# Three passes of rounded parts for the mixer's products with v and with the state in the second layer of a four-layer hybrid model

## The chip, the cores and the metric

The kernel runs on one core of one Trainium2 chip. The metric is the device time of one execution in microseconds (us), lower is better; a kernel's time is the median of its runs. The outputs are fp32.

## What is computed

The model has four layers on 1040 tokens (16 meta tokens and 1024 tokens of input) of width 1024: sliding-window attention, an mLSTM, an HGRN2 and attention again. Each layer projects the normed input, mixes over time, gates, and projects back. The change is in the second layer, whose mixer does this for each of 8 heads and for each block of 128 tokens in turn:

```python
def step(carry, inp):                      # mlstm_chunkwise, one block
    C, n, m = carry
    q_, k_, v_, li, lf = inp
    ...
    qk = jnp.einsum('bhtd,bhsd->bhts', q_, k_) * jnp.exp(D - m_t[..., None])
    num = w_inter[..., None] * jnp.einsum('bhtd,bhde->bhte', q_, C) + jnp.einsum('bhts,bhse->bhte', qk, v_)
    den = w_inter * jnp.einsum('bhtd,bhd->bht', q_, n) + qk.sum(axis=-1)
    h = num / jnp.maximum(jnp.abs(den), jnp.exp(-m_t))[..., None]
    ...
    C_new = w_old[..., None, None] * C + jnp.einsum('bhs,bhsd,bhse->bhde', w_s, k_, v_)
```

q and k have 128 columns a head, v has 256. After it, h is multiplied by a sigmoid gate, normed over the head's 256 columns, multiplied by a silu gate and projected by w_out.

## The kernel before, in words

**Staging.** Activations lie with features on the partitions and tokens along the row. Tokens go in three chunks (400, 384, 256) for projections and in nine blocks (16, then eight of 128) for mixers. A projection (`proj` L212, `proj_v` L249, `proj_out` L297) takes both operands as two rounded parts in fp32r, high and low: `split` (L194) makes the high part with ScalarE and the remainder with VectorE, and three passes (high·high, high·low, low·high) are accumulated in one PSUM bank (L231, L281, L326). Weights come by DMA in halves of 512 columns into `raw` (two buffers, L207), and are split into `wh` and `wl` (three buffers each). All DMAs of the layer are issued by SyncE, in order.

**Order.** TensorE's order is written out by hand: lists of steps, each with a cost in nanoseconds, a function that issues it, and perhaps a function `pre` that loads its weights, called as soon as the steps ahead cost less than 12 us (`LOOKAHEAD`). `weave` (L58) merges two lists in proportion to their costs. The other engines' instructions are put in order by the framework's scheduler, by priority; steps wrapped in `hi` (L290) get a priority 40 places earlier.

**The mixer** (`mixer`, L980). `start` loads the head's two decay rows, spread over all 128 partitions (`rb` and `wb`, 1040 columns each, one buffer each, L986 and L987). Then for block b:

- `s1(b)`: q·k on TensorE (L994), k transposed (L996), the decay matrix E (L998 on VectorE, L1000 on ScalarE), W = E times q·k (L1004), qw = q times the row of `wb` (L1007), kw = the transposed k scaled by a column of E (L1012, ScalarE).
- `s2(b)`: num = W·v (L1019) + qw·C (L1021), 257 columns: 256 of v and one of ones that gives the denominator; then the division (L1023 to L1029).
- `s3(b)`: kw·v (L1035), and the new state C = old C times a scalar + that product (L1038 and L1040, VectorE; two buffers).
- `s4(b)`: the result transposed back (L1049, L1051).

The steps go s1(b), s2(b-1), s3(b-1), s4(b-2). All three products L1019, L1021 and L1035 have fp32 operands. A head's mixer list, without its last three steps, is woven with the projections of the next head (q, k, v). The last three are woven with the first six steps of the gate part: `gates` (L1114) gives the two sigmoid-gate projections (`og_proj`, L1065) one after the other, then a silu-gate projection with the three norm statistics (`stat`, L1088) put into it. The second silu gate and `proj_out` follow. For head 6 the last three mixer steps are held over to head 7, whose mixer is woven with head 6's gates. The squares of the first sigmoid-gate half stay in a row of their own, `sqr` (L1076), until the second half adds to it (L1082).

Of the kernel before, what the change touches and what calls it, by code (L numbers as in the profile page):

```python
# [9 lines left out]
F32 = mybir.dt.float32  # L10
F32R = mybir.dt.float32r
# [4 lines left out]
P = 128  # L16
# [57 lines left out]
def flat(groups):  # L74
    return [x for grp in groups for x in grp]
# [38 lines left out]
def hybrid_kernel(ctx: ExitStack, tc: tile.TileContext, ins, out, layers=(0, 1, 2, 3)):  # L114
# [13 lines left out]
    def nm(x):  # L128
        ctr[0] += 1
        return f"{x}{ctr[0]}"  # L130
# [16 lines left out]
    def psum(tag, bufs):  # L147
        return ps.tile([P, 512], F32, tag="p", name=nm(tag), bufs=8)
# [141 lines left out]
    def hi(fn):  # L290
        def f():
            with tc.high_priority(offset=PRIO):
                fn()

        return f
# [567 lines left out]
    def layer_b(i, j, fin):  # L863
# [107 lines left out]
        def v_evac(h):  # L971
            def f(acc, b, c0, cn):
                R["v", h, b] = V = vtile()
                put_v(V, acc, b, cn)
                if h == 0:
                    gate_evac(acc, b, cn)
                g.memset(V[:cn, 256:257], 1.0)
            return f

        def mixer(h):  # L980
            W = {}

            def start():
                R["h", h, 0], R["h", h, 1] = row(), row()
                R["rb"], R["wb"] = (R["mix"].tile([P, T], F32, tag=z, name=nm(z), bufs=1) for z in ("rb", "wb"))
                sp.dma_start(R["rb"], R["rows_d"][0, h].partition_broadcast(P))  # L986
                sp.dma_start(R["wb"], R["rows_d"][1, h].partition_broadcast(P))  # L987

            def s1(b):
                mix, q, k = R["mix"], R["q", h], R["k", h]  # L990
                c0, cn = blk(b)
                cs = slice(c0, c0 + cn)
                pq = psum("pm", 2)
                pe.matmul(pq[:cn, :cn], k[:, cs], q[:, cs], start=True, stop=True)  # L994
                if b < NB - 1:
                    pe.transpose(pq[:cn, 128:256], k[:, cs], ident)  # L996
                W["E", b] = E = mix.tile([P, P], F32, tag="E", name=nm("E"), bufs=2)
                v.scalar_tensor_tensor(E[:cn, :cn], R["rb"][:cn, cs], R["bcol"][:cn, b, h : h + 1],  # L998
                                       R["caus"][:cn, :cn], op0=ALU.add, op1=ALU.add)
                s.activation(E[:cn, :cn], E[:cn, :cn], AF.Exp)  # L1000
                W["W", b] = w = mix.tile([P, P], F32, tag="W", name=nm("W"), bufs=2)
                if b == 0:
                    g.memset(w, 0.0)
                v.tensor_tensor(w[:cn, :cn], E[:cn, :cn], pq[:cn, :cn], op=ALU.mult)  # L1004
                if b:
                    W["qw", b] = qw = mix.tile([P, P], F32, tag="qw", name=nm("qw"), bufs=2)
                    v.tensor_tensor(qw, q[:, cs], R["wb"][:, cs], op=ALU.mult)  # L1007
                if b < NB - 1:
                    W["kw", b] = kw = mix.tile([P, P], F32, tag="kw", name=nm("kw"), bufs=2)
                    if b == 0:  # L1010
                        g.memset(kw, 0.0)
                    s.activation(kw[:cn], pq[:cn, 128:256], AF.Identity, scale=E[:cn, cn - 1 : cn])  # L1012

            def s2(b):
                mix = R["mix"]
                c0, cn = blk(b)
                V = R["v", h, b]
                num = psum("po", 1)
                pe.matmul(num[:, :257], W["W", b], V[:, :257], start=True, stop=(b == 0))  # L1019
                if b:  # L1020
                    pe.matmul(num[:cn, :257], W["qw", b], W["C"][:, :257], start=False, stop=True)  # L1021
                den = small(1)
                s.activation(den[:cn], num[:cn, 256:257], AF.Abs)  # L1023
                v.tensor_tensor(den[:cn], den[:cn], R["em"][:cn, b, h : h + 1], op=ALU.max)
                v.reciprocal(den[:cn], den[:cn])
                W["hn", b] = hn = mix.tile([P, 256], F32, tag="hn", name=nm("hn"), bufs=2)
                if b == 0:
                    g.memset(hn, 0.0)
                s.activation(hn[:cn], num[:cn, :256], AF.Identity, scale=den[:cn])  # L1029

            def s3(b):
                mix = R["mix"]
                c0, cn = blk(b)
                pc = psa()
                pe.matmul(pc[:, :257], W["kw", b], R["v", h, b][:, :257], start=True, stop=True)  # L1035
                Cn = mix.tile([P, 258], F32, tag="C", name=nm("C"), bufs=2)
                if b == 0:
                    v.tensor_copy(Cn[:, :257], pc[:, :257])  # L1038
                else:
                    v.scalar_tensor_tensor(Cn[:, :257], W["C"][:, :257], R["wb"][:, c0 + cn - 1 : c0 + cn],  # L1040
                                           pc[:, :257], op0=ALU.mult, op1=ALU.add)
                W["C"] = Cn

            def s4(b):
                c0, cn = blk(b)
                cs = slice(c0, c0 + cn)
                pt = psum("pt", 1)
                for c in range(2):
                    pe.transpose(pt[:, c * P : c * P + P], W["hn", b][:, c * P : c * P + P], ident)  # L1049
                for c in range(2):  # L1050
                    v.tensor_copy(R["h", h, c][:, cs], pt[:, c * P : c * P + cn])  # L1051

            steps = [[0.0, start, None]]
            for b in range(NB + 2):
                if b < NB:
                    steps.append([320, hi(lambda b=b: s1(b)), None])
                if 0 <= b - 1 < NB:
                    steps.append([856, hi(lambda b=b - 1: s2(b)), None])
                    if b - 1 < NB - 1:
                        steps.append([428, hi(lambda b=b - 1: s3(b)), None])  # L1060
                if 0 <= b - 2 < NB:
                    steps.append([214, hi(lambda b=b - 2: s4(b)), None])
            return steps

        def og_proj(h):  # L1065
            st = {}

            def evac(c):
                def f(acc, n, c0, cn):
                    cs = slice(c0, c0 + cn)  # L1070
                    hr = R["h", h, c]
                    a = sigmoid_from(acc[:, :cn], cn)
                    v.tensor_tensor(hr[:, cs], hr[:, cs], a[:, :cn], op=ALU.mult)
                    if c == 0:
                        if n == 0:
                            R["sqr"] = R["mix"].tile([P, T], F32, tag="sqr", name=nm("sqr"), bufs=1)  # L1076
                        R["sq", n] = q = R["sqr"][:, cs]
                        s.activation(q, hr[:, cs], AF.Square)
                    else:
                        q = R["sq", n]  # L1080
                        s.activation(a[:, :cn], hr[:, cs], AF.Square)
                        v.tensor_tensor(q, q, a[:, :cn], op=ALU.add)  # L1082
                        R["sqs", n] = qs = [tpool.tile([P, 400], F32R, tag=z, name=nm(z), bufs=YS)[:, :cn]
                                            for z in ("yh", "yl")]
                        split(q, *qs)
                return f

            def stat(n, c0, cn):  # L1088
                def fn():
                    cs = slice(c0, c0 + cn)  # L1090
                    q = R["sq", n]
                    sm = psa()
                    for i, z in enumerate(R["sqs", n]):
                        pe.matmul(sm[:, :cn], R["ones"], z, start=(i == 0), stop=(i == 1))
                    rstd_from(sm, q, cn, 256)
                    for c in range(2):
                        hr = R["h", h, c]
                        v.scalar_tensor_tensor(hr[:, cs], hr[:, cs], R["hgain"][:, 2 * h + c : 2 * h + c + 1], q,
                                               op0=ALU.mult, op1=ALU.mult)
                return [2 * cn * MM, fn, None]  # L1100

            g0, g1 = (proj(win[8 * h + 4 + c], evac(c)) for c in range(2))
            return g0, g1, [stat(n, *CHUNKS[n]) for n in range(3)]
# [10 lines left out]
        def gates(h):  # L1114
            g0, g1, stats = og[h]
            tail = flat(zg[h][0])
            for n in (2, 1, 0):
                later(tail, (7000.0, stats[n]))
                tail = g1[n] + tail
            return flat(g0) + tail  # L1120

        head = [list(vg[0][n]) for n in range(3)]
        for n in (0, 1):
# [521 lines left out]
```

## Time and profile before

| | |
|---|---|
| runs of the kernel before | 2597.77, 2593.03, 2597.73 us; median 2597.73 |
| the profiled execution | 2594.76 us, its span 2593.0 us |
| second layer, first to last matmul of its mixers | about 544 to 1457 us of the span |
| one head of it (start of one mixer to the next) | 132.8 us, of which the mixer takes about 63 |

The span is what the profiler saw from the first to the last instruction. Engines are PE (TensorE's matmuls), PEld (its weight loads), DVE (VectorE), ACT (ScalarE), POOL (GpSimd), SP (SyncE). A busy time of PE counts each matmul from its start to its modelled end, so neighbours overlap; how much time one really takes on TensorE is seen from the distance between starts, or from the chain of waits, where pieces follow one another. A product with fp32 operands leaves two records, a pass in fp32r one.

### The profile page before, as it was taken

The numbers are of one execution on the slowest core, as the hardware profiler recorded it, in microseconds if no ns is written. First come the engines' busy times: TensorE is split into PE (matmuls) and PEld (weight loads), VectorE is DVE, ScalarE is ACT, GpSimd is POOL, SyncE is SP. The second block draws the span as 40 slices with busy tenths as digits, with TensorE's granted clock in tenths as the row PEclk, the third lists the DMA queues.
The fourth block names the chain that finished last, engine by engine and source line by source line (L and its number), as shares of the span: only waits on it lengthen the run. The fifth ranks groups of instructions, "written<-read, shape, count | busy, mean of one in ns | idle before, by whom it ended". The sixth has DMA issues, their size and how long they took to land.

```text
span 2593.0 us, 54342 instructions
## 1 busy us (share of the span) xinstructions
PE 2547.2 (98%) x20446; PEld 2487.2 (96%) x20446; DVE 1949.5 (75%) x5266; ACT 1682.9 (65%) x4403; POOL 243.4 (9%) x564
## 2 busy tenths in 40 slices
PE   8999999999999999999999999999999999999999
PEld 8899999999999999999999999999999999999999
DVE  7897898785657474747475688978878978887996
ACT  8766766576464555555555757877676857767772
POOL 0321231000000000000000000001000000321330
PEclk9999999999999999999999999999999999999999
DMA  5223212021111111111111111111111113212112
GB/s 157 62 66 95 57 43 70 29 67 54 46 50 49 51 41 58 42 50 45 53 42 50 58 35 34 35 35 35 34 42 34 35 51 93 64 43 82 56 42 78
DMA packets 86058, 140.21 MB, mean 54 GB/s; under 512 B 12425, under 2 KB 39186, under 8 KB 85794
## 3 DMA queue, kind: packets, MB, share of 16 engines
q1 hardware_dynamic: 85794, 136.73, 17.1%
q8 instruction: 161, 2.64, 0.4%
q14 instruction: 103, 0.84, 0.1%
HBM read 121.83 MB, written 4.27 MB: 49 GB/s over the span
## 4 chain that ended last, share of the span: by engine, by line
PE 62%; DVE 13%; ACT 8%; issue 2%; DMA 1%; SPq 0%; POOL 0%; DVEq 0%; ACTq 0%; POOLq 0%
PE pj L231 28%; PE pj L326 14%; PE pj L281 10%; DVE wl L196 1%; PE po L1019 1%; PE po L1021 1%; PE pa L1035 1%; ACT X L1269 1%; PE po L773 1%; DVE x L329 1%; PE pj L277 1%; ACT Sm L737 1%; PE pt L755 1%; DVE Sm L734 1%; DVE X L1267 1%
## 5 line engine op out<-in xcount | busy, mean ns | idle before, releaser
L231 PE MATMUL pj<-uh,wh 128*128 128x256 f32 (+2 forms) x2688 | 915.7, 341 | 7.7 <-ACT uh L401 7.2
L231 PE MATMUL pj<-ul,wh 128*128 128x256 f32 (+2 forms) x2688 | 864.3, 322 | 0.3
L231 PE MATMUL pj<-uh,wl 128*128 128x256 f32 (+2 forms) x2688 | 864.6, 322 | 0.0
L231 PEld LDWEIGHTS pj<-uh,wh 128*128 128x128 f32 x2688 | 508.5, 189 | 17.4 <-ACT uh L401 7.2
L231 PEld LDWEIGHTS pj<-ul,wh 128*128 128x128 f32 x2688 | 508.8, 189 | 6.4 <-DVE ul L196 0.8
L231 PEld LDWEIGHTS pj<-uh,wl 128*128 128x128 f32 x2688 | 507.9, 189 | 0.0
L196 DVE TENSOR_TENSOR wl<-wr,wh 128x512 fp32r<-128x512 f32 (+1 forms) x338 | 234.2, 703 | 55.0 <-ACT wh L195 52.1
L195 ACT CAST wh<-wr 128x512 fp32r<-128x512 f32 (+1 forms) x338 | 202.7, 613 | 97.6 <-PE pj L326 31.5
L326 PE MATMUL pj<-yh,wh 128*128 128x384 f32 (+2 forms) x768 | 253.6, 330 | 9.8 <-DVE x L329 8.3
L329 DVE TENSOR_TENSOR x<-x,pj 128x384 f32<-128x384 f32 (+2 forms) x480 | 233.8, 507 | 33.4 <-PE pj L326 32.1
L326 PE MATMUL pj<-yh,wl 128*128 128x384 f32 (+2 forms) x768 | 246.2, 321 | 0.0
L326 PE MATMUL pj<-yl,wh 128*128 128x384 f32 (+2 forms) x768 | 246.2, 321 | 0.0
L281 PE MATMUL pj<-wh,uh 128*128 128x256 f32 (+1 forms) x768 | 232.7, 303 | 0.0
L281 PE MATMUL pj<-wl,uh 128*128 128x256 f32 (+1 forms) x768 | 216.3, 282 | 0.0
L281 PE MATMUL pj<-wh,ul 128*128 128x256 f32 (+1 forms) x768 | 215.9, 281 | 0.0
L737 ACT ACTIVATE Sm<-Sm,s 128x257 f32<-128x257 f32 (+2 forms) x272 | 131.1, 483 | 88.6 <-DVE s L734 86.3
L740 POOL TENSOR_TENSOR Sm<-Sm,s 128x512 f32<-128x512 f32 (+2 forms) x136 | 139.3, 1024 | 406.5 <-DVE s L739 386.3
L458 ACT ACTIVATE t<-t 128x384 f32<-128x384 f32 (+2 forms) x240 | 118.0, 491 | 75.5 <-DVE t L457 74.6
L195 ACT CAST yh<-r 128x384 fp32r<-128x384 f32 (+2 forms) x120 | 57.0, 478 | 156.2 <-PE pj L326 139.4
L326 PEld LDWEIGHTS pj<-yh,wh 128*128 128x128 f32 x768 | 144.9, 189 | 14.0 <-DVE x L329 10.3
L457 DVE SCALAR_TENSOR_TENSOR t<-pj,t 128x400 f32<-128x400 f32 (+2 forms) x168 | 86.3, 513 | 81.5 <-ACT t L456 80.2
L281 PEld LDWEIGHTS pj<-wh,uh 128*128 128x128 f32 x768 | 144.7, 188 | 2.2
(303 smaller groups left out, 5447.1 us busy)
## 6 DMA issues: line engine op xcount, KB each, us to landing
wr<-in_b_win SPq DMA_DIRECT2D x124, 256.0 KB, 2.8
wr<-in_a_win SPq DMA_DIRECT2D x80, 256.0 KB, 2.8
wr<-in_c_win SPq DMA_DIRECT2D x64, 256.0 KB, 3.0
wr<-in_a_wout SPq DMA_DIRECT2D x32, 256.0 KB, 2.8
wr<-in_b_wout SPq DMA_DIRECT2D x32, 256.0 KB, 2.7
t<-t SPq DMA_DIRECT2D x100, 48.0 KB, 1.9
cs<-in_rope SPq DMA_DIRECT2D x11, 400.0 KB, 3.7
cs<-in_rope SPq DMA_DIRECT2D x11, 384.0 KB, 3.5
```

The costliest lines, as they stand in the source:

```text
L195: s.copy(h, src)
L196: v.tensor_tensor(l, src, h.bitcast(F32), op=ALU.subtract)
L231: pe.matmul(acc[:, :cn], a[:, k, :], b[:, k, c0 : c0 + cn], start=(k == 0 and i == 0), stop=(k == KT - 1 and i == 2))
L277: pe.matmul(acc[:48, :nc], um[0][:, k, :], m[:, kk, :], start=(k == 0 and m is wh), stop=(k == KT - 1 and m is wl))
L281: pe.matmul(acc[:cn, :nc], a[:, k, c0 : c0 + cn], m[:, kk, :], start=(k == 0 and j == 0), stop=(k == KT - 1 and j == 2))
L326: pe.matmul(acc[:, :cn], a[:, k, mc], b, start=(k == 0 and i == 0), stop=(k == 1 and i == 2))
L329: v.tensor_tensor(x[:, m, c0 : c0 + cn], x[:, m, c0 : c0 + cn], acc[:, :cn], op=ALU.add)
L457: v.scalar_tensor_tensor(a[:, :cn], z, 0.0, a[:, :cn], op0=ALU.min, op1=ALU.subtract)
L458: s.activation(a[:, :cn], a[:, :cn], AF.Exp)
L734: v.tensor_tensor_reduce(Sm[:nq, u, :nk], S[:nq, u, :nk], R["masks"][:nq, P + mo : P + mo + nk], rq, sinks[u], ALU.add, ALU.min, st[:nq, u ...
L737: s.activation(Sm[:nq, u, : nk + 1], Sm[:nq, u, : nk + 1], AF.Exp, scale=-1.0, bias=st[:nq, u : u + 1], accum_out=den[:nq, u : u + 1])
L740: g.tensor_tensor(Sm[:nq, :, :nk], Sm[:nq, :, :nk], den[:nq].rearrange("p (u c) -> p u c", c=1).to_broadcast([nq, 2, nk]), op=ALU.mult)
```

## The change

The three products with v and with the state run as three passes over rounded parts, with 258 columns in place of 257 (the ones column is doubled). For this v, W, qw and C are split by `split`, and kw is made as two parts: ScalarE writes the high part in place of kw, VectorE the remainder. The low parts and high parts have tiles of their own (two buffers, for C one), and C is updated in place. The decay rows come block by block (`fetch`, both rows of 128 columns in one DMA, three buffers, block b+1 asked for in s1(b)) in place of `rb` and `wb`, the row `sqr` goes (its use is taken by the rotating buffers of `tmp`), and the two sigmoid gates alternate chunk by chunk in place of one after the other. The costs of s2 and s3 in the list go from 856 and 428 to 714 and 357.

```diff
             def start():
                 R["h", h, 0], R["h", h, 1] = row(), row()
-                R["rb"], R["wb"] = (R["mix"].tile([P, T], F32, tag=z, name=nm(z), bufs=1) for z in ("rb", "wb"))
-                sp.dma_start(R["rb"], R["rows_d"][0, h].partition_broadcast(P))
-                sp.dma_start(R["wb"], R["rows_d"][1, h].partition_broadcast(P))
+                fetch(0)
+
+            def fetch(b):
+                c0, cn = blk(b)
+                W["rw", b] = z = R["mix"].tile([P, 2, P], F32, tag="rw", name=nm("rw"), bufs=3)
+                sp.dma_start(z[:, :, :cn], R["rows_d"][:, h, c0 : c0 + cn].partition_broadcast(P))
+
+            def parts(z, cols=P, bufs=2):
+                return [R["mix"].tile([P, cols], F32R, tag=z + q, name=nm(z + q), bufs=bufs) for q in "hl"]
+
+            def product(acc, a, c, start, stop):
+                for i, (x0, x1) in enumerate(((0, 0), (0, 1), (1, 0))):
+                    pe.matmul(acc, a[x0], c[x1][:, :258], start=(start and i == 0), stop=(stop and i == 2))
 
             def s1(b):
 ...
+                if b + 1 < NB:
+                    fetch(b + 1)
+                rb, wb = (W["rw", b][:, z, :cn] for z in range(2))
+                W["V", b] = parts("V", 258)
+                split(R["v", h, b][:, :258], *(z[:, :258] for z in W["V", b]))
 ...
-                W["W", b] = w = mix.tile([P, P], F32, tag="W", name=nm("W"), bufs=2)
+                w = mix.tile([P, P], F32, tag="W", name=nm("W"), bufs=2)
 ...
                 v.tensor_tensor(w[:cn, :cn], E[:cn, :cn], pq[:cn, :cn], op=ALU.mult)
+                W["W", b] = parts("W")
+                split(w, *W["W", b])
                 if b:
-                    W["qw", b] = qw = mix.tile([P, P], F32, tag="qw", name=nm("qw"), bufs=2)
-                    v.tensor_tensor(qw, q[:, cs], R["wb"][:, cs], op=ALU.mult)
+                    qw = mix.tile([P, P], F32, tag="W", name=nm("qw"), bufs=2)
+                    v.tensor_tensor(qw, q[:, cs], wb, op=ALU.mult)
+                    W["qw", b] = parts("qw")
+                    split(qw, *W["qw", b])
 ...
-                    s.activation(kw[:cn], pq[:cn, 128:256], AF.Identity, scale=E[:cn, cn - 1 : cn])
+                    last = E[:cn, cn - 1 : cn]
+                    s.activation(kh[:cn], pq[:cn, 128:256], AF.Identity, scale=last)
+                    v.scalar_tensor_tensor(kl[:cn], pq[:cn, 128:256], last, kh[:cn].bitcast(F32),
+                                           op0=ALU.mult, op1=ALU.subtract)
 
             def s2(b):
 ...
-                pe.matmul(num[:, :257], W["W", b], V[:, :257], start=True, stop=(b == 0))
+                product(num[:, :258], W["W", b], W["V", b], True, b == 0)
                 if b:
-                    pe.matmul(num[:cn, :257], W["qw", b], W["C"][:, :257], start=False, stop=True)
+                    product(num[:, :258], W["qw", b], W["Cs"], False, True)
 ...
             def s3(b):
 ...
-                pe.matmul(pc[:, :257], W["kw", b], R["v", h, b][:, :257], start=True, stop=True)
-                Cn = mix.tile([P, 258], F32, tag="C", name=nm("C"), bufs=2)
+                product(pc[:, :258], W["kw", b], W["V", b], True, True)
                 if b == 0:
-                    v.tensor_copy(Cn[:, :257], pc[:, :257])
+                    W["C"] = mix.tile([P, 258], F32, tag="C", name=nm("C"), bufs=1)
+                C = W["C"][:, :258]
+                if b == 0:
+                    v.tensor_copy(C, pc[:, :258])
                 else:
-                    v.scalar_tensor_tensor(Cn[:, :257], W["C"][:, :257], R["wb"][:, c0 + cn - 1 : c0 + cn],
-                                           pc[:, :257], op0=ALU.mult, op1=ALU.add)
-                W["C"] = Cn
+                    v.scalar_tensor_tensor(C, C, W["rw", b][:, 1, cn - 1 : cn], pc[:, :258], op0=ALU.mult, op1=ALU.add)
+                W["Cs"] = parts("C", 258, 1)
+                split(C, *(z[:, :258] for z in W["Cs"]))
 ...
-                    steps.append([856, hi(lambda b=b - 1: s2(b)), None])
+                    steps.append([714, hi(lambda b=b - 1: s2(b)), None])
                     if b - 1 < NB - 1:
-                        steps.append([428, hi(lambda b=b - 1: s3(b)), None])
+                        steps.append([357, hi(lambda b=b - 1: s3(b)), None])
 ...
                     if c == 0:
-                        if n == 0:
-                            R["sqr"] = R["mix"].tile([P, T], F32, tag="sqr", name=nm("sqr"), bufs=1)
-                        R["sq", n] = q = R["sqr"][:, cs]
+                        R["sq", n] = q = tmp()[:, :cn]
 ...
             def stat(n, c0, cn):
 ...
-                    q = R["sq", n]
+                    q = tmp()[:, :cn]
 ...
             for n in (2, 1, 0):
                 later(tail, (7000.0, stats[n]))
-                tail = g1[n] + tail
-            return flat(g0) + tail
+                tail = g0[n] + g1[n] + tail
+            return tail
```

More of the change, by code (lines that the diff above doesn't have):

```diff
@@ L976, in f @@
                     gate_evac(acc, b, cn)
-                g.memset(V[:cn, 256:257], 1.0)
+                g.memset(V[:cn, 256:258], 1.0)
             return f
@@ L997, in s1 @@
                 W["E", b] = E = mix.tile([P, P], F32, tag="E", name=nm("E"), bufs=2)
-                v.scalar_tensor_tensor(E[:cn, :cn], R["rb"][:cn, cs], R["bcol"][:cn, b, h : h + 1],
+                v.scalar_tensor_tensor(E[:cn, :cn], rb[:cn], R["bcol"][:cn, b, h : h + 1],
                                        R["caus"][:cn, :cn], op0=ALU.add, op1=ALU.add)
                 s.activation(E[:cn, :cn], E[:cn, :cn], AF.Exp)
-                W["W", b] = w = mix.tile([P, P], F32, tag="W", name=nm("W"), bufs=2)
+                w = mix.tile([P, P], F32, tag="W", name=nm("W"), bufs=2)
                 if b == 0:
@@ L1004, in s1 @@
                 v.tensor_tensor(w[:cn, :cn], E[:cn, :cn], pq[:cn, :cn], op=ALU.mult)
+                W["W", b] = parts("W")
+                split(w, *W["W", b])
                 if b:
-                    W["qw", b] = qw = mix.tile([P, P], F32, tag="qw", name=nm("qw"), bufs=2)
-                    v.tensor_tensor(qw, q[:, cs], R["wb"][:, cs], op=ALU.mult)
+                    qw = mix.tile([P, P], F32, tag="W", name=nm("qw"), bufs=2)
+                    v.tensor_tensor(qw, q[:, cs], wb, op=ALU.mult)
+                    W["qw", b] = parts("qw")
+                    split(qw, *W["qw", b])
                 if b < NB - 1:
-                    W["kw", b] = kw = mix.tile([P, P], F32, tag="kw", name=nm("kw"), bufs=2)
+                    W["kw", b] = kh, kl = parts("kw")
                     if b == 0:
-                        g.memset(kw, 0.0)
-                    s.activation(kw[:cn], pq[:cn, 128:256], AF.Identity, scale=E[:cn, cn - 1 : cn])
+                        for z in (kh, kl):
+                            g.memset(z.bitcast(F32), 0.0)
+                    last = E[:cn, cn - 1 : cn]
+                    s.activation(kh[:cn], pq[:cn, 128:256], AF.Identity, scale=last)
+                    v.scalar_tensor_tensor(kl[:cn], pq[:cn, 128:256], last, kh[:cn].bitcast(F32),
+                                           op0=ALU.mult, op1=ALU.subtract)
             def s2(b):
@@ L1016, in s2 @@
                 c0, cn = blk(b)
-                V = R["v", h, b]
                 num = psum("po", 1)
-                pe.matmul(num[:, :257], W["W", b], V[:, :257], start=True, stop=(b == 0))
+                product(num[:, :258], W["W", b], W["V", b], True, b == 0)
                 if b:
-                    pe.matmul(num[:cn, :257], W["qw", b], W["C"][:, :257], start=False, stop=True)
+                    product(num[:, :258], W["qw", b], W["Cs"], False, True)
                 den = small(1)
```

## The prediction, as it stood before the result

> **What bounds the kernel now.** I read the page first (busy shares), then the busy time by stretches, then the chain of waits inside one mixer, then the groups of instructions, the waits and single instructions by time.
>
> ```profile
> PE 2547.2 (98%) x20446; PEld 2487.2 (96%) x20446; DVE 1949.5 (75%) x5266; ACT 1682.9 (65%) x4403; POOL 243.4 (9%) x564
> ...
> 540.00:1460.00 920.00, 919.46 (x6119) 905.40 (x6118) 555.65 (x1435) 510.69 (x1220) 12.52 (x89) 1.00 0.15 49
> ...
> 666.60:700.00 33.40, 33.40 (x219) 32.74 (x219) 24.34 (x70) 22.62 (x57) 0.39 (x4) 1.00 0.17 53
> 700.00:730.00 30.00, 30.00 (x231) 29.24 (x230) 11.47 (x41) 10.86 (x31) 1.14 (x8) 1.00 0.14 44
> ...
> 544.00:598.00 54.00, 53.46 (x383) 51.46 (x382) 35.85 (x114) 34.06 (x93) 1.53 (x12) 1.00 0.15 46
> 666.60:730.00 63.40, 63.40 (x448) 61.98 (x448) 35.81 (x110) 33.48 (x87) 1.53 (x12) 1.00 0.15 48
> ...
> 1398.20:1457.00 58.80, 58.80 (x368) 56.91 (x368) 39.15 (x114) 41.90 (x104) 0.00 (x0) 1.00 0.11 37
> ```
>
> The columns after the stretch are its length, then PE, PEld, DVE, ACT and POOL, each with its instructions, then the granted clock. In the second layer's 920 us TensorE is idle for 0.54 us, at full clock. So there a microsecond of TensorE's work taken away is one gained, as long as nobody makes TensorE wait; and a wait added is lost in full. The second thing to see is how uneven the others are: VectorE is busy for 24.34 of the first 33.4 us of head 1's mixer (73%), for 11.47 of the next 30 (38%). The first head's mixer (544 to 598) and the last one's (1398 to 1457) are the fullest of the eight.
>
> **What the products cost, and what three passes will.** The chain of waits inside head 1's mixer, with start, duration and count:
>
> ```profile
> 701.07 2.84 PE pj L281 x24
> 703.91 0.44 PE pa L1035 x2
> 704.35 1.43 PE pj L281 x12
> ...
> 707.75 0.43 PE po L1019 x2
> 708.18 0.43 PE po L1021 x2
> 708.62 2.84 PE pj L281 x24
> ...
> 715.73 0.43 PE po L1021 x2
> ```
> ```profile
> L1019 PE MATMUL po<-v,W 128*128 128x257 f32 x144 | 43.1, 380 | 0.0
> L1021 PE MATMUL po<-C,qw 128*128 128x257 f32 x128 | 38.3, 380 | 0.5 <-DVE C L1040 0.5
> L1035 PE MATMUL pa<-v,kw 128*128 128x257 f32 x128 | 38.2, 379 | 0.0
> ```
>
> A full-precision product takes two records and, from the step to its neighbour (708.62 less 707.75, halved; 704.35 less 703.91), 0.435 us. An fp32r pass of 256 columns takes 2.84/24 = 0.1183 us, each with weights of its own. By the column 258 take 0.1193 us, three passes 0.358 us. A product saves 0.077 us. The records are two to a product: (144 + 128 + 128)/2 = 200 products. **200 x 0.077 = 15.4 us** off TensorE.
>
> The Trainium skill, page "FP8 and Floating Point Precision", section "TensorE Precision Notes", counts four passes for true fp32. By its 4 to 3 alone a quarter of 0.435 us, 0.109 us a product and 21.8 us in all, would go. The measured 0.1183 us a pass keeps it at 15.4, since a pass of its own costs more than a quarter of 0.435.
>
> **What is added to the other engines.** The nearest rows:
>
> ```profile
> L195 ACT CAST yh<-r 128x400 fp32r<-128x400 f32 x12 | 6.3, 524 | 7.5 <-DVE r L476 7.5
> L195 ACT CAST yh<-r 128x256 fp32r<-128x256 f32 x12 | 4.9, 407 | 45.0 <-PE pj L326 45.0
> ...
> L196 DVE TENSOR_TENSOR yl<-r,yh 128x256 fp32r<-128x256 f32 x12 | 5.1, 425 | 8.9 <-ACT yh L195 8.8
> L1007 DVE TENSOR_TENSOR qw<-q,wb 128x128 f32<-128x128 f32 x62 | 17.2, 286 | 32.4 <-PE po L1021 18.9 <-DMA wb<-rowsd 13.3
> L998 DVE SCALAR_TENSOR_TENSOR E<-rb,bcol,caus 128x128 f32<-128x128 f32 x63 | 21.7, 344 | 10.5 <-ACT kw L1012 10.3
> ```
>
> A head splits v 9 times, W 9, qw 8, C 8 times, and gets 8 remainders of kw. VectorE: 17 x 0.425 + 17 x 0.286 + 8 x 0.344 = 14.8 us. ScalarE: 17 x 0.407 for 258 columns and 17 x 0.30 for 128 (an estimate: 0.407 less 128 times the 0.81 ns a column between the two rows) = 12.0 us; kw's high part replaces kw. Beside a mixer of 63.4 us this lifts VectorE from 35.8 to 50.6 (80%) and ScalarE from 33.5 to 45.5 (72%). Both fit, so these 118 and 96 us lie beside TensorE's work. But in the first 33.4 us of that mixer six blocks pass s1 and four s3: VectorE gets 6 x 0.425 + 6 x 0.286 + 5 x 0.286 + 6 x 0.344 + 4 x 0.425 = 9.5 us on top of 24.3, more than there is. Projection work that nobody waits for (the next head's k) must slip into the emptier second half. In the first head VectorE comes to 50.7 of 54, in the last one both come to 54 of 58.8.
>
> **The path that gets longer.** One chain returns to TensorE within a block: kw·v, the new C, then qw·C of the next block. W, qw, kw and v are ready a period (about 7.5 us, 708.18 to the next at 715.73) ahead, and their splits have that long. C's has not:
>
> ```profile
> 558.58 0.48 DVE L1040 SCALAR_TENSOR_TENSOR C<-C,wb,pa 128x257 f32<-128x257 f32 x1
> 559.12 0.70 PE L1021 MATMUL po<-C,qw 128*128 128x257 f32 x2 [0.54 <-DVE C L1040]
> 570.58 0.48 DVE L1040 SCALAR_TENSOR_TENSOR C<-C,wb,pa 128x257 f32<-128x257 f32 x1
> 571.92 0.60 PE L1021 MATMUL po<-C,qw 128*128 128x257 f32 x2
> ...
> 689.56 0.48 DVE L1040 SCALAR_TENSOR_TENSOR C<-C,wb,pa 128x257 f32<-128x257 f32 x1
> 691.45 0.60 PE L1021 MATMUL po<-C,qw 128*128 128x257 f32 x2
> ...
> 726.92 0.48 DVE L1040 SCALAR_TENSOR_TENSOR C<-C,wb,pa 128x257 f32<-128x257 f32 x1 [2.73 <-PE pa L1035]
> 728.80 0.60 PE L1021 MATMUL po<-C,qw 128*128 128x257 f32 x2
> 1419.20 0.53 ACT L195 CAST yh<-sqr 128x400 fp32r<-128x400 f32 x1 [0.64 <-DVE sqr L1082]
> 1419.76 0.57 DVE L196 TENSOR_TENSOR yl<-sqr,yh 128x400 fp32r<-128x400 f32 x1 [0.20 <-ACT yh L195]
> ```
>
> The last two rows show a split: 0.03 us from the end of the cast to the start of the subtraction. After C, the low part is there 0.03 + 0.407 + 0.03 + 0.425 + 0.03 = 0.92 us later, if both engines are free. The low part is used first in the second pass, 0.12 us after the product's start, and W·v ahead of it is 0.08 shorter, so the old slack counts almost whole. It is 691.45 less 690.04 = 1.41 us in head 1's third block and 1.40 us in its last one: both just hold 0.92 and one wait of half a microsecond. I followed all 64 in time: heads 1 to 6 have these two, and the other six slacks of a head are longer. In the fuller half I expect one stall of about 0.5 us a head: 3 us for six heads. In head 0 TensorE already waits, at 559.12, and the next but one slack there is 571.92 less 571.06 = 0.86 us, below 0.92: 2 us. In head 7 the engines are nearly full: 1 us. **Stalls: 6 us**, an estimate, bounded by nothing (all chains meet free engines) and by 20 us (each of the 64 finds one operation of about 0.3 us ahead of it).
>
> **What else moves.** The order of the sigmoid gates asks for the second one's weights 6.4 us sooner, by the costs in the list (two chunks, 640 columns, of the first one now come behind it). They are loaded and split in 2.8 us (the DMA row below) plus two operations of about 0.7 us; what covers them is the first chunk, 4 us by its cost. I take nothing, at most 2 us a head. The rotating buffer that replaces `sqr` is held for one chunk: nothing, or a wait of one sigmoid step, below 1 us a head.
>
> ```profile
> wr<-in_b_win SPq DMA_DIRECT2D x114, 256.0 KB, 2.8
> rb<-rowsd SPq DMA_DIRECT2D x7, 520.0 KB, 3.4
> ...
> SPq L207 <- DVE wl L196: 385.5, 87, 13.2
> SPq L987 <- DVE C L1040: 132.7, 7, 19.6
> ```
>
> SyncE's queue: today `wb`'s load blocks it up to 19.6 us a head, weights behind it. That wait goes, and gains at most the 0.54 us of idle TensorE. Added are 72 small loads. One (128 KB) should land within the 2.8 us of a 256 KB load, and s1 of the next block comes 7.5 us later. I take nothing; the other end is the third rival.
>
> **Sum.** The profiled execution is 2594.76 us, 1.76 above its span, and 2.97 below the median of 2597.73. 2594.76 - 15.4 + 6 = 2585.4. Half of the way to the median, 1.5 us, is added, since a new median can lie at either place: **2587 us**.
>
> **The rivals.**
>
> 1. No stall that counts: every split falls into a gap. 2594.8 - 15.4 = 2579.4, at the median's offset up to 2582. For it: six slacks in eight are longer than what a free engine needs. Against: the 0.54 us already there, and a VectorE over 100% in the first halves.
> 2. VectorE and ScalarE become the bound in the mixers: stalls of 12 to 25 us, 2591 to 2604 (2597.73 is inside). For it: 54 of 58.8 us in head 7 on both, 50.7 of 54 in head 0, and waits in order come on top of busy time. Against: 20% free in the six others.
> 3. Slower: a row load stands in SyncE's queue behind a weight load that waits for its buffer. Such waits last up to 13.2 us. It decides once a wait passes 7.5 - 2.8 = 4.7 us: then E's instruction on VectorE waits, with the head's C behind it, whose slack is 1.4 us at the shortest. The longest gives 13.2 - 4.7 - 1.4 = 7.1 us; once a head, 57 us: 2636. For it: the queue is in order and blocked for long. Against: 385.5/87 = 4.4 us is the mean, and the loads have the higher priority of s1.
> 4. Slower too: weight loads that don't hide. Three passes load weights three times, a product now twice.
>
> ```profile
> 704.31 0.19 PEld L281 LDWEIGHTS pj<-wh,ul 128*128 128x128 f32 x1
> 704.42 0.28 PE L281 MATMUL pj<-wh,ul 128*128 128x256 f32 x1
> 704.42 0.19 PEld L281 LDWEIGHTS pj<-wh,uh 128*128 128x128 f32 x1
> ```
>
> With 0.19 us a load in the open, 200 more loads are 38 us: 2594.8 - 15.4 + 38 = 2617. The rows speak against it: the next load starts 0.11 us after the one before, beside the matmul of that one, though each takes 0.19. The Trainium skill, page "TensorE: Matmul & The Clock Gate", section "The mechanism", says that loads overlap running matmuls only where the row groups differ; by that rule this would be the outcome, and these full-height rows do not bear it out.
> 5. The parts don't run as single passes but at full precision: 3 x 0.435 in place of 0.435, 174 us slower. The tiles have the type of `uh` and `wh`, whose passes leave one record of 0.118 us each; hardly possible.
>
> **How the numbers follow.** Chances: forecast (2580 to 2593) 0.52, no stall 0.18, bound by the others 0.14, blocked rows 0.13, loads in the open 0.02, full precision 0.01. The range leaves out the last three (0.16) and holds the second rival's times: 2577 to 2605. A measurement of this kernel tells 0.2% (5.2 us) from no change, so faster means below 2592.5. That holds for the forecast but its upper end, and for no stall: 0.68. Within 0.2%: most of the second rival and that upper end, 0.12. Slower: rivals 3 to 5 and the second one's end, 0.20.
>
> **What would show it.** The chain of waits in a mixer should hold pieces of three matmuls of 0.36 us at the places of the old 0.43. Idle time of PE, ended by VectorE's low part of C, should sum to 3 to 9 us, most of it in the first head, the last one and the first halves. VectorE should read near 80% and ScalarE near 72% in a middle mixer. E should not wait for a DMA. It is wrong if the passes come at over 0.13 us, if TensorE idles over 12 us in the layer, or if waits for the row loads appear.

## The result and the profile after

The changed kernel takes 2600.82 us (median of 22 runs), the one before 2596.14 us in the same sessions: a ratio of 1.0019, 95% interval 1.0012 to 1.0026. It is slower, by about 5 us, where 2587 was forecast. The profiled execution took 2599.31 us.

The page of the changed kernel, and its busy time in the second layer's stretch (length, then PE, PEld, DVE, ACT, POOL, then the granted clock):

```profile
span 2597.5 us, 55485 instructions
PE 2541.0 (98%) x20646; PEld 2488.2 (96%) x20646; DVE 2034.6 (78%) x5602; ACT 1744.6 (67%) x4675; POOL 244.2 (9%) x572
```
```profile
540.00:1460.00 920.00, 907.15 (x6268) 900.82 (x6267) 634.58 (x1758) 565.74 (x1479) 12.22 (x94) 0.99 0.21 48
```

The stretch in which TensorE was idle for 0.54 us now has 12.85 us of idle time. VectorE got 79 us more in it, ScalarE 55 us. The clock reads 0.99 in place of 1.00; that small figure matters below. (The granted clock is the share of TensorE's full clock that it was allowed; in the stretches called half-clock below it reads 0.50.) Line numbers are now those of the changed kernel: L997 is a pass of a product, L1013 makes E, L1024 qw, L1064 C.

The chain of waits in head 1, away from stalls, and three rows of TensorE's waits in the whole execution (total us, times, longest), for the high part of C, its low part and the high part of W (`Ch`, `Cl`, `Wh`; the low part of W is `Wl`):

```profile
724.51 0.72 PE po L997 x6
725.23 2.85 PE pj L281 x24
728.08 0.36 PE pa L997 x3
```
```profile
PE po L997 <- ACT Ch L195: 5.5, 5, 2.0
PE po L997 <- DVE Cl L196: 3.6, 7, 1.1
PE po L997 <- ACT Wh L195: 3.2, 1, 3.2
```

A product is 0.36 us, as forecast. So TensorE's work did shrink, and the gain was lost in waits for the high and low parts.

The clearest view is the time from the first q·k of one head to that of the next, read from the starts of those matmuls in the trace. It needs no model of where a matmul ends:

| us | head 0 to 1 | heads 1 to 6, mean of the five steps |
|---|---|---|
| before | 122.25 | 132.79 |
| after | 135.53 | 132.44 |

Head 0 lost 13.3 us. The later heads gained 0.35 us each, where 25 products of 0.077 us should have given 1.9. All the idle time lies in these heads: 9.08 us in head 0, 3.77 us in heads 1 to 5 together, and 0.01 us from head 6's start to the layer's end, though head 7's mixer was to be the fullest of all by the prediction. The execution hides part of the loss: its second layer began 2.9 us earlier than in the one before (first q·k at 541.4 against 544.3 us). Two half-clock stretches of 3.4 us each, from 345.1 and 403.1 us in the earlier profile, do not stand in this one.

**Head 0.** Instructions by time, and the clock by stretches:

```profile
545.10 0.15 DVE L1019 TENSOR_TENSOR W<-E,pm 16x16 f32<-16x16 f32 x1
546.26 0.27 DVE L1019 TENSOR_TENSOR W<-E,pm 128x128 f32<-128x128 f32 x1
547.21 0.29 ACT L195 CAST Wh<-W 128x128 fp32r<-128x128 f32 x1
547.55 0.58 PE L997 MATMUL po<-Vh,Wh 128*128 128x258 f32 x1 [3.16 <-ACT Wh L195]
```
```profile
541.00:546.00 5.00, 3.39 (x23) 2.89 (x21) 3.31 (x10) 3.86 (x10) 0.00 (x0) 1.00 0.18 52
546.00:552.00 6.00, 4.07 (x12) 3.74 (x13) 5.58 (x20) 5.67 (x18) 0.00 (x0) 0.55 0.14 45
552.00:558.00 6.00, 4.57 (x25) 4.35 (x24) 3.98 (x13) 3.31 (x9) 0.10 (x1) 0.88 0.16 44
558.00:564.00 6.00, 4.33 (x15) 4.13 (x16) 5.76 (x17) 4.66 (x15) 0.00 (x0) 0.72 0.00 0
```

The first W was ready at 545.25, but its cast started at 547.21: ScalarE had other activations and the convolution work of the next head's q ahead of it in its order. TensorE stood still for 3.16 us, from 544.39 to 547.55. The granted clock fell within this wait, 2.2 us after it began, and stayed at 0.50 until 553.45:

```profile
544.39:546.62 2.23, 0.00 (x0) 0.00 (x0) 2.14 (x7) 1.80 (x5) 0.00 (x0) 1.00 0.00 0
546.62:547.55 0.93, 0.00 (x0) 0.00 (x0) 0.60 (x2) 0.93 (x4) 0.00 (x0) 0.50 0.36 95
```

A pass of 258 columns took 0.42 us instead of 0.28 by its record; passes of 400 columns started every 0.33 us instead of every 0.18. The later waits in this head (2.04 us for C's high part and 1.06 us for its low part, up to 560.06; 1.99 and 0.45 us, up to 605.18) came with two more such stretches, of 3.4 us each. In all the trace has 13.65 us at half clock in head 0, and TensorE was busy in 11.9 us of it. By the distances 0.18 and 0.33 us some 45% of that, about 5.4 us, was lost (an estimate), on top of the 9.08 us of idle time. The Trainium skill, page "TensorE: Matmul & The Clock Gate", section "HAM oscillation — how this bites in real kernels", warns of idle gaps over about 3.4 us. Here a gap of 3.2 us was enough, and so were gaps of 2.0 us with a shorter one (1.06 or 0.45 us) close behind.

**The end of each head.** VectorE in head 1's last blocks, and what TensorE and the chain make of it:

```profile
730.71 0.28 DVE L1024 TENSOR_TENSOR qw<-q,rw 128x128 f32<-128x128 f32 x1
...
735.75 0.35 DVE L1013 SCALAR_TENSOR_TENSOR E<-rw,bcol,caus 128x128 f32<-128x128 f32 x1 [2.70 <-DMA rw<-rowsd]
736.02 0.48 DVE L1064 SCALAR_TENSOR_TENSOR C<-C,rw,pa 128x258 f32<-128x258 f32 x1
...
738.53 0.42 DVE L196 TENSOR_TENSOR Cl<-C,Ch 128x258 fp32r<-128x258 f32 x1
```
```profile
731.02 4.70 DMA rw<-rowsd
...
739.00 0.50 PE po L997 x2
```
```profile
rw<-rowsd SPq DMA_DIRECT2D x61, 128.0 KB, 4.3
```

The E at 735.75 belongs to block 1 of the next head: VectorE's order has it ahead of this head's last C. Its row load was issued as soon as the head's last qw (730.71) had freed a row buffer, and landed 4.7 us later. C came behind it. ScalarE waited in the same way for that E's exponential, and then had two casts of weights ahead of C's. In the whole layer E waited for its rows 29 times, where in the kernel before it never did:

```profile
DVE E L1013 <- DMA rw<-rowsd: 48.4, 29, 3.2
```

The row loads (128 KB in 512-byte pieces) land after 4.3 us, the weights' 256 KB after 2.8.

### The profile page after: what moved, and what is told of

The parts are those of the page before. It is cut to its first block, busy times and chain, and to the rows that moved or that the text cites. A ratio compares the mean times of both kernels' runs of the same rounds, so it can differ in the third digit from the quotient of the medians.

```text
span 2597.5 us, 55485 instructions
## 1 busy us (share of the span) xinstructions
PE 2541.0 (98%) x20646; PEld 2488.2 (96%) x20646; DVE 2034.6 (78%) x5602; ACT 1744.6 (67%) x4675; POOL 244.2 (9%) x572
## 4 chain that ended last, share of the span: by engine, by line
PE 61%; DVE 14%; ACT 9%; DMA 4%; issue 2%; SPq 0%; POOL 0%; DVEq 0%; ACTq 0%
PE pj L231 29%; PE pj L326 14%; PE pj L281 8%; DMA rw<-rowsd 2%; DVE wl L196 2%; PE po L997 1%; PE po L773 1%; PE pt L755 1%; ACT Sm L737 1%; DVE Sm L734 1%; ACT wh L195 1%; ACT X L1291 1%; PE pj L277 1%; PE pa L997 1%; DVE x L329 1%
## 5 line engine op out<-in xcount | busy, mean ns | idle before, releaser
L231 PE MATMUL pj<-uh,wh 128*128 128x256 f32 (+2 forms) x2688 | 903.6, 336 | 6.9 <-ACT uh L401 6.4
L281 PE MATMUL pj<-wh,uh 128*128 128x256 f32 (+1 forms) x768 | 222.8, 290 | 0.0
L326 PEld LDWEIGHTS pj<-yl,wh 128*128 128x128 f32 x768 | 144.9, 189 | 0.7 <-DVE yl L196 0.2
```

Source lines behind the costliest of these rows:

```text
L231: pe.matmul(acc[:, :cn], a[:, k, :], b[:, k, c0 : c0 + cn], start=(k == 0 and i == 0), stop=(k == KT - 1 and i == 2))
L281: pe.matmul(acc[:cn, :nc], a[:, k, c0 : c0 + cn], m[:, kk, :], start=(k == 0 and j == 0), stop=(k == KT - 1 and j == 2))
L326: pe.matmul(acc[:, :cn], a[:, k, mc], b, start=(k == 0 and i == 0), stop=(k == 1 and i == 2))
```

## The experiments

The theory from these readings: the passes save what was forecast, and the gain is lost in two places, the row loads through three buffers and the first head's casts, which stand behind other work in the engines' order. The rival: VectorE and ScalarE are simply too full with the splits. Each kernel is compared with the kernel before on the same chip. The heads' times are read as in the table above, from one profiled execution of each kernel; head 0 of e4 holds more work than the others (see there).

| | ratio to before, 95% interval | head 0 to 1, us | later heads, us |
|---|---|---|---|
| e1 rows by block, nothing else | 1.0055, 1.0043 to 1.0067 | 126.12 | 134.69 |
| e2 gates alternating, nothing else | 1.0003, 0.9994 to 1.0012 | 122.31 | 132.82 |
| e3 changed kernel, four row buffers | 0.9991, 0.9981 to 1.0000 | 131.85 | 131.48 |
| e4 changed kernel, first head later | 1.0028, 1.0017 to 1.0038 | 134.87 | 132.36 |
| e5 changed kernel, constant operands | 0.9943, 0.9928 to 0.9959 | 122.82 | 130.95 |
| e6 as e1, four row buffers | 1.0014, 1.0005 to 1.0022 | 123.96 | 132.84 |
| e7 as e3, first head's steps earlier in order | 0.9958, 0.9943 to 0.9973 | 124.00 | 131.46 |
| e8 as e3, a lag in the first head | 0.9975, 0.9965 to 0.9984 | 130.26 | 131.52 |
| e9 as e7, three row buffers | 1.0011, 1.0003 to 1.0020 | 132.75 | 132.33 |
| e10 as e7, and a lag | 0.9956, 0.9943 to 0.9970 | 123.10 | 131.49 |

### e1: the rows alone

```diff
-                R["rb"], R["wb"] = (R["mix"].tile([P, T], F32, tag=z, name=nm(z), bufs=1) for z in ("rb", "wb"))
...
+                W["rw", b] = z = R["mix"].tile([P, 2, P], F32, tag="rw", name=nm("rw"), bufs=3)
+                sp.dma_start(z[:, :, :cn], R["rows_d"][:, h, c0 : c0 + cn].partition_broadcast(P))
```

> The kernel before with one part of the change alone: the decay rows come block by block through three buffers; products stay at full precision, nothing is split. Theory (the passes save about 14.5 us; of it and more is given back where the next head's E waits on VectorE for its row load with the last C of the head behind it, and where the first head's products wait for their casts): E waits here too, some 2.5 us at each head's end, but C's slack of 1.4 us takes most of it: 0 to +5 us against before. Rival (the stalls come from VectorE and ScalarE being too full with the splits): no idle time of TensorE beyond the 0.5 us of before, 0 +- 1 us.

Measured: 14.4 us slower (2606.56 against 2592.13), where 0 to 5 was expected. The place was right, the size was not: C's slack did not cover it. The waits of this kernel and two rows of VectorE:

```profile
DVE E L1004 <- DMA rw<-rowsd: 120.9, 45, 4.1
```
```profile
729.41 0.35 DVE L1004 SCALAR_TENSOR_TENSOR E<-rw,bcol,caus 128x128 f32<-128x128 f32 x1 [3.93 <-DMA rw<-rowsd]
...
730.53 0.46 DVE L1046 SCALAR_TENSOR_TENSOR C<-C,rw,pa 128x257 f32<-128x257 f32 x1
```

E waits for its rows in 45 of 72 blocks, in the middle of the heads too, and holds up VectorE each time. Before, E never waited for a load. Without a single split, every later head takes 1.9 us longer. The rival's 0 is out.

### e2: the gates alone

```diff
-                        R["sq", n] = q = R["sqr"][:, cs]
+                        R["sq", n] = q = tmp()[:, :cn]
...
-                tail = g1[n] + tail
-            return flat(g0) + tail
+                tail = g0[n] + g1[n] + tail
+            return tail
```

> The kernel before with another part alone: the two sigmoid gates alternate by chunk and the row for their squares is replaced by rotating buffers. Theory: same time, 0 +- 1.5 us. A rival that puts the loss here (weights of the second gate late, rotating buffers short) expects +5 us or more and idle time of TensorE after each head's v projection.

Measured: 1.0003, no change, and the heads' times are those of before. This part costs nothing that can be told from noise (interval 0.9994 to 1.0012).

### e3: four row buffers

```diff
-                W["rw", b] = z = R["mix"].tile([P, 2, P], F32, tag="rw", name=nm("rw"), bufs=3)
+                W["rw", b] = z = R["mix"].tile([P, 2, P], F32, tag="rw", name=nm("rw"), bufs=4)
```

> The changed kernel with four row buffers in place of three. Theory: the next head's second row load no longer has to wait for the last qw of the head, E and C come on time, TensorE's idle time at the heads' ends goes: 6 to 11 us less than the changed kernel, so 4 us or more below the kernel before. Rival (engines too full): within 2 us of the changed kernel.

Measured: 0.9991 of before against the changed kernel's 1.0019, some 7 us gained by one number in the code, as the theory had it against the changed kernel; the 4 us below the kernel before were not reached (1.4). E's waits for rows and TensorE's waits now:

```profile
DVE E L1013 <- DMA rw<-rowsd: 2.9, 6, 0.6
```
```profile
PE po L997 <- ACT Wh L195: 3.4, 1, 3.4
PE po L997 <- ACT Ch L195: 2.0, 1, 2.0
PE po L997 <- DVE Cl L196: 1.1, 1, 1.1
PE po L997 <- DVE Wl L196: 0.4, 1, 0.4
```

The later heads take 1.3 us less than before the change, 1.0 us less than in the changed kernel. All waits that this view still lists are in head 0, one of each kind.

### e4: the first head later, with more work beside it

```diff
-        body = flat(qg[0]) + flat(kg[0]) + flat(qg[1])
+        body = flat(qg[0]) + flat(kg[0]) + qg[1][0]
...
+                if h == 0 and b == 1:
+                    steps.append([2000.0, lambda: None, None])
...
-                body += weave(mx, (flat(qg[h + 1]) if h else []) + flat(kg[h + 1]) + flat(vg[h + 1]))
+                body += weave(mx, flat(qg[h + 1] if h else qg[1][1:]) + flat(kg[h + 1]) + flat(vg[h + 1]))
```

> The changed kernel with the first head's mixer given more room: two of the three chunks of the next head's q projection are woven into it, and 2000 ns of its list lie between its second s1 and its first W times v. Theory: the 3.2 us wait for the cast of W, the C waits after it and the half-clock stretches that follow them (some 10 us at half speed) go: 6 to 12 us less than the changed kernel. Rival (engines too full): the waits move to a later block of the same head, within 3 us of the changed kernel.

A miss: 1.0028, no better than the changed kernel, where 6 to 12 us were expected. This kernel's first q·k:

```profile
543.11 0.24 PE L1009 MATMUL pm<-q,r 128*16 128x16 f32 x2 [7.16 <-DVE r L967]
```

The edit took away two of the three chunks of the q projection that stood between k's projection and the mixer, so TensorE waited 7.16 us for k's own convolution, with a half-clock stretch of 10.2 us. It is a new wait of the edit's making, and the total decides nothing between the theories. The head's own time says a little more. The two chunks are 48 passes, about 7.1 us at full clock by the distances between their starts in the changed kernel (24 of 0.176 and 24 of 0.118 us), and they now lie inside head 0. Its 134.87 us hold that much more work in less than the changed kernel's 135.53; the wait for W's cast is gone, and TensorE is idle in the head for 4.2 us in place of 9.1.

### e5: the passes by themselves

```diff
-                product(num[:, :258], W["W", b], W["V", b], True, b == 0)
+                product(num[:, :258], R["cw"], R["cv"], True, b == 0)
...
-                    product(num[:, :258], W["qw", b], W["Cs"], False, True)
+                    product(num[:, :258], R["cw"], R["cv"], False, True)
...
-                product(pc[:, :258], W["kw", b], W["V", b], True, True)
+                product(pc[:, :258], R["cw"], R["cv"], True, True)
```

The splits are left out as well.

> The changed kernel without its splits: the three products run as the same three passes in the same places, but on constant tiles in place of v, W, qw, kw and C, so TensorE waits for none of them and the mixer's result is not the reference's (kw is made as in the kernel before, unused). Theory: the passes alone save 0.072 us a product (the trace of the changed kernel away from its waits), 200 times, 14.5 us: 0.9945 of the kernel before. Rival (passes on these tiles are no cheaper than full precision, the gain was never there): 0.998 or more.

Measured: 2578.48 against 2593.89, 15.4 us less, 0.9943. A later head takes 130.95 us, 1.84 less than before: 0.074 us for each of its 25 products. The gain in the sum is real, and this is what it is worth with hardly a wait (TensorE is idle for 1.75 us in the layer). That the total meets 15.4 to the decimal is luck: the interval goes from 10.6 to 18.7 us.

### e6: the rows alone, with four buffers

One number differs from e1.

> The first experiment (full precision, decay rows by block) with four row buffers in place of three. Theory (a row load waits for a buffer that only the block in work frees, and takes 4.3 us to land): most of its loss of 14 us goes, 0 to +4 us against the kernel before. Rival (the loss comes from the loads being many and small, or from SyncE's queue): it stays, +8 us or more.

Measured: 1.0014, 2.3 us slower than before by the medians (2596.16 against 2593.89), 3.6 by the ratio, in the theory's range. The number and size of the loads are those of e1, so neither is the cause by itself; the ring of three is. What is left is in head 0 (123.96 against 122.25 us); the later heads take the time of before, though E still waits there:

```profile
DVE E L1004 <- DMA rw<-rowsd: 52.4, 24, 3.8
```

### e7: the first head's steps earlier in the other engines' order

```diff
-    def hi(fn):
+    def hi(fn, prio=PRIO):
         def f():
-            with tc.high_priority(offset=PRIO):
+            with tc.high_priority(offset=prio):
...
+            pr = 250 if h == 0 else PRIO
...
-                    steps.append([320, hi(lambda b=b: s1(b)), None])
+                    steps.append([320, hi(lambda b=b: s1(b), pr), None])
```

The same for s2, s3 and s4, and four row buffers.

> The changed kernel with four row buffers, and the first head's mixer steps ordered 250 places earlier in place of 40 on the other engines, so that its casts stand ahead of the convolution work of the next head's q. Theory (in head 0 the casts stand behind that work in ScalarE's and VectorE's order): the waits of 3.4, 0.4, 2.0 and 1.1 us there and their half-clock stretches go or shrink below 2 us; 6 to 10 us below the four-buffer kernel, 0.996 of the kernel before. Rival (the two engines are simply too full there): waits of the same size elsewhere in head 0, within 2 us of the four-buffer kernel.

Measured: 2581.11 against 2593.89, 0.9958: faster than both kernels. Head 0 falls from 131.85 to 124.00 us, with the same instructions on the same engines. What TensorE still waits for:

```profile
PE po L997 <- DVE Cl L196: 0.7, 2, 0.5
PE pj L281 <- ACT q L959: 0.5, 1, 0.5
PE po L997 <- ACT Wh L195: 0.5, 1, 0.5
```

No half-clock stretch is left in head 0. So the engines were not too full; the order was wrong. The rival is out for head 0. The order's 7.9 us there contain what the half clock took in e3's head 0, which this experiment does not part from the waits themselves.

### e8: a lag in the first head

e3 with the 2000 ns step of e4, and no other move.

> The changed kernel with four row buffers, and 2000 ns of the list left between the first head's second s1 and its first W times v, with no other move. Theory: W's cast has its time (the wait of 3.4 us and its half clock go, some 7 us), but the blocks behind come closer and the waits for C grow by 1 to 3 us: 3 to 6 us below the four-buffer kernel. Rival (too full): the wait only moves, within 2 us of the four-buffer kernel.

Measured: 0.9975, some 4 us below e3, within the 3 to 6 us of the theory. The trace bears only part of it out: head 0 takes 130.26 us, 1.6 us less than in e3. W's cast has its time; the next wait takes its place, longer than I expected, with 6.8 us at half clock behind it:

```profile
556.16 0.38 PE L997 MATMUL po<-Ch,qwh 128*128 128x258 f32 x1 [3.21 <-ACT Ch L195]
```

### e9: the earlier order with three buffers

> The changed kernel with three row buffers as it was, and only the first head's earlier order (250 places). Theory (two separate losses that add): it keeps the heads' ends losing some 1.2 us each and the end of head 0 its 2.4 us wait with half clock; it gains the 6 to 10 us that the order alone was worth with four buffers: 0.998 to 0.9995 of the kernel before. Rival (the row loads' waits set everything, the order only helps once they are gone): 1.001 or more, as the changed kernel.

Measured: 1.0011, the rival's value; the theory's range ends below the interval. The two losses do not add: the order is worth about 8 us with four buffers (e3 to e7) and 2 us with three (the changed kernel to this one), and these 2 us are not clear of noise. In this kernel head 0 waits for a row load at its end, as the later heads do. Its matmul, and the chain ahead of it:

```profile
605.82 0.39 PE L997 MATMUL po<-Ch,qwh 128*128 128x258 f32 x1 [3.33 <-ACT Ch L195]
```
```profile
598.97 4.74 DMA rw<-rowsd
...
604.34 0.61 ACT wh L195
...
606.26 0.35 DVE Cl L196
```

Head 0 takes 8.75 us more than in e7. This wait, the 0.45 us behind it and the half-clock stretch of 3.4 us that follows (some 1.3 us lost, worked out as above) make about 5.1 of them. Some 2 us more is idle time in shorter waits, the longest of 1.1 us; what is left was not followed.

### e10: order and lag

> Four row buffers, the earlier order in the first head, and 1500 ns of the list ahead of its first W times v. Theory: the order alone left about 2 us of waits in head 0, of which the lag can take the 0.5 us for the first cast and may add as much for C: within 2 us of the kernel with order and four buffers, 0.996 of the kernel before. Rival (head 0 is still short of room): 2 us or more faster than that.

Measured: 0.9956 (five runs), the same as e7. Head 0 is not short of room once its order is right.

## Why the prediction was wrong, step by step

- **What bounds the kernel** held: TensorE in the second layer, with 0.54 us of slack. What the change saved came through where no wait was added: in e5, and in the changed kernel's heads 6 and 7 (from head 6's first q·k to the last instruction 1258.4 us in place of 1262.5; their 50 products make 3.9).
- **200 x 0.077 = 15.4 us** held: 0.074 us a product in e5's later heads, and 15.4 us in its total, whose interval is wide.
- **The added work of 118 and 96 us beside TensorE's** held. VectorE's new groups in the changed kernel (busy time, mean of one in ns):

```profile
L196 DVE TENSOR_TENSOR Vl<-v,Vh 128x258 fp32r<-128x258 f32 x70 | 29.5, 421 | 3.2 <-ACT Vh L195 3.0
L196 DVE TENSOR_TENSOR Cl<-C,Ch 128x258 fp32r<-128x258 f32 x63 | 26.7, 424 | 3.3 <-ACT Ch L195 2.0
L196 DVE TENSOR_TENSOR Wl<-W,Wh 128x128 fp32r<-128x128 f32 x72 | 20.5, 284 | 3.5 <-ACT Wh L195 3.5
L1034 DVE SCALAR_TENSOR_TENSOR kwl<-pm,E,kwh 128x128 fp32r<-128x128 f32 x56 | 19.3, 344 | 0.0
L196 DVE TENSOR_TENSOR qwl<-qw,qwh 128x128 fp32r<-128x128 f32 x64 | 18.0, 282 | 0.0
```

  They make 114 us, the forecast durations to 4 ns. The engine's busy time rose by 79 us only: instructions that follow one another closely overlap in their records (E and C at 735.75 and 736.02 above), and such time counts once. So the forecast shares came out too high: in head 1's mixer VectorE is busy for 46.8 of 63.4 us (74%, not 80) and ScalarE for 41.2 (65%, not 72). And the splits do lie beside TensorE's work: e7 has all of them and waits for little.
- **"I take nothing" for the 72 row loads** is the step that failed first. I read their landing from a load of twice the size (2.8 us) and found 4.3, and I followed neither who frees the row buffers nor what E's place in VectorE's order does across the border of two heads. A wait for the row loads was named as a sign of being wrong, and it came, 29 times; so did the other sign that was seen, more than 12 us of idle time (12.85). The step is worth 14 us by itself (e1) and about 7 us beside the splits (e3 against the changed kernel).
- **"Stalls: head 0: 2 us"** failed as well. I followed C alone and wrote that W, qw, kw and v are ready a period ahead. In a head's first block W·v comes without a period before it, in head 0 of the kernel before 2.8 us after its q·k (544.3 and 547.1 us), and only the first head has the convolutions of two projections still in the queues; the first and longest wait was for W's cast. Head 0 lost 13.3 + 1.9 = 15.2 us, where 2 were forecast.
- **No price for the clock.** Nothing in the sum said that a wait of 2 to 3 us can bring 3.4 to 6.8 us at half clock. In head 0 that is about 5.4 of the 15.2 us; the added idle time is 8.5 of them, and the last 1.3 us were not followed.
- **Heads 1 to 6, 0.5 us each from queueing:** the size came to 1.5 us (132.44 against e5's 130.95), and 1.0 of it had another cause, the row load. With four buffers 0.5 us is left (131.48 against e5's 130.95). That this equals the forecast stall is luck: e3's TensorE is idle for 0.13 us in heads 1 to 5 together, so the slacks of 1.4 us do hold, and where the 0.5 us goes stays open. **Head 7: 1 us** came to nothing.
- **The third rival** named the right instruction (E on VectorE, C behind it) and the wrong cause: not SyncE's queue behind weight loads, but a buffer that the head's own last qw frees. It was given 0.13 and a far larger price.
- The other rivals: weight loads in the open and full precision fell with the 0.36 us product. That VectorE and ScalarE become the bound gives the right time, 2591 to 2604, for a reason that e7 refutes; head 7, where it was to show most, has no idle time.

Left open: e7 is some 4 us above e5 by their ratios, with intervals that overlap; in the traces head 0's 1.2 us and the later heads' 0.5 us each make about 4. Which split costs it was not tried. Nor was a kernel with whole rows and splits.

## What to carry to other kernels

When a change buys TensorE time with work on other engines, find the first place where its new operand is needed with no lead, here the first block of the first head, and count what stands ahead of the new instruction in that engine's order; the mean load of the engine does not tell. When a large buffer is cut into a ring of small ones, count who holds each slot at the border of two loops, and what stands behind the instruction that waits for the next one. A priority and one more buffer, here 1 KB a partition, turned 5 us lost into 11 us gained (by the ratios).

## What the runs showed of the hardware

- In the changed kernel a wait of TensorE of 2.0 us (with 0.45 us more behind it) brought 3.4 us at half clock, one of 3.2 us 6.8 us. The length of the wait alone does not tell: one of 3.3 us brought 3.4 us (e9), one of 3.2 us 6.8 us (e8), one of 1.7 us with 0.45 us behind it none (e4, the second ending at 607.5 us). The two stretches around the first of these in the changed kernel:

```profile
601.00:604.30 3.30, 1.35 (x12) 1.14 (x10) 1.55 (x4) 1.66 (x5) 0.00 (x0) 1.00 0.23 39
604.30:607.80 3.50, 3.01 (x10) 2.81 (x11) 2.12 (x8) 1.52 (x5) 0.10 (x1) 0.55 0.95 122
```

- A load of 128 KB in 512-byte pieces, spread over 128 partitions from two rows, landed after 4.3 us; one of 256 KB in pieces of 2048 bytes after 2.8.
- Three fp32r passes of 258 columns with weights of their own take 0.36 us, a full-precision product of 257 takes 0.435: about a sixth less.
